# Two block products for a pair of token blocks and weight tiles: seven instead of eight, in the second projection stage of a two-layer encoder

## The chip, the cores and the metric

The kernel runs on one core of a Trainium2 chip. A core has four engines that compute, each with its own queue of instructions, worked off in order: TensorE (PE in the profile, its weight loads PEld), VectorE (DVE), ScalarE (ACT) and GpSimd (POOL). SyncE (SP) computes nothing; here it issues most of the transfers (DMA) between the chip's main memory (DRAM) and the on-chip memory SBUF. TensorE writes its results to PSUM, a second on-chip memory, from where VectorE and ScalarE read them. The metric is the device time of one execution in microseconds.

## The reference

One inference step of a two-layer encoder over 2048 prompt tokens and 32 sampled ones, 1024 features wide. Layer one is a gated DeltaNet; its result h is projected to shared keys and values and, in layer two, to queries and gates of a sliding-window attention:

```python
kv = h @ w_kv                                   # 256 key columns, 256 value columns
k  = rope_partial(kv[..., :256]); v = kv[..., 256:]
proj = h @ b_w_in                               # 1024 query columns, 1024 gate columns
q  = rope_partial(proj[..., :1024]) * 64 ** -0.5
z  = proj[..., 1024:]
o  = banded_attention(q, k, v, sinks)           # own chunk of 64 tokens and two chunks back
y  = layer_norm(4 ** 0.25 * h + (o * silu(z)) @ b_w_out, ln_g, ln_b)
```

The change is mainly in how k, q, z and v are projected, the second projection stage.

## The kernel before

All large products are made in float32 precision from pieces that TensorE reads: a tile x is split into a high part (x cast to the type fp32r, by ScalarE) and a low part (x less its high part, by VectorE or GpSimd), and x·w becomes three matmuls, high·high, high·low and low·high. `project` (L75) makes one block so: a tile of 128 weight columns, all eight slices of 128 features, a block of TB = 416 tokens, 24 matmuls into one PSUM bank. There are NB = 5 blocks of tokens; block 4 holds the end of the prompt and the 32 sampled tokens.

The order of the kernel: the first projection stage (class `P1`), the DeltaNet's chunks (`Delta`) with its output projection and layer norm beside them (`O1`), the second projection stage (class `P2`), attention (`Attention`) with its output projection, and a tail that normalises the last rows.

The second stage, as it stands before: `P2.load` (L321) fetches a block of h, transposed, from DRAM and splits it; all five blocks then lie in SBUF. Weight tiles are numbered here 0 and 1 (keys), 2 to 9 (queries), 10 to 17 (gates 0 to 7). While the last rows of the DeltaNet are projected, gates 0 and 1 of the first blocks are made; then gates 0 and 1 of blocks 2 to 4; then the values (`values`, L352): 128 tokens at a time as the stationary operand against 256 value columns, with the 32 tokens left over in each block collected over four blocks; then keys and queries (`rotated`, L1395), each with the rotation in `rope` (L1340), while the output weights of layer two are split and written to DRAM beside it (L1080); then gates 2 and 3 of all blocks and gates 4 to 7 of blocks 2 to 4. Each weight tile is fetched and split once and used on all its blocks. Eight gate blocks are left for attention's first steps, where they fill TensorE while the first scores and softmaxes run (L2053).

`rope` is, per block of 128x416: ScalarE copies from PSUM (L1345), VectorE shuffles rows (L1346), GpSimd multiplies by the sine (L1347), VectorE multiplies by the cosine (L1348) and adds (L1349). `gate` (L1422) is a tanh and a copy on ScalarE and one VectorE instruction.

What sets the order: from L2033 on the second stage is put in order by the framework's planner; attention's order (L2091) is the one written. PSUM banks come from two pools in turn (L1332).

The tail (L1605) applies mean, scale and the two tables to the last 128 rows in two halves on VectorE, after the Newton steps for the inverse deviation (L513, L515), and stores the halves.

## Time and profile before

| what | value |
| --- | --- |
| median of 3 runs (2111.22 to 2111.9) | 2111.88 us |
| profiled execution | 2112.2 us |
| its span, first to last instruction | 2110.4 us |
| TensorE busy, share of the span | 98% |
| VectorE, ScalarE, GpSimd busy | 62%, 43%, 40% |
| granted TensorE clock | 0.997 |
| moved by DMA | 307.78 MB, 145 GB/s to and from main memory |

Rows in the profile read so: a line of kernel.py (L79), the engine, the operation, output and inputs by the program's names, shapes as partitions x elements, then times. A timeline row begins with start and duration in us. Matmul durations overlap, since TensorE pipelines them; what a matmul costs in a row of them is the distance between their starts.

### The profile page before, as it was taken

The page shows a single profiled execution, that of the slowest core. Times are in us where ns is not written, and L with a number is a line of the kernel's source. Part 1 is how long each engine was busy: PE and PEld are TensorE (multiplying, and loading weights), DVE is VectorE, ACT ScalarE, POOL GpSimd, SP SyncE. Part 2 cuts the span into 40 slices and gives each one's busy share as a digit, 9 for nine tenths or more (in the row PEclk, how much of TensorE's full clock was granted, in tenths as well). Part 3 has the DMA queues.
Part 4 walks back from the last instruction along what each step waited for, and adds up shares of the span by engine and source line. Part 5 has one row for each costly group of instructions (what it writes and reads, how often), then busy time and mean ns, then how long its engine had stood idle before and what let it go on. Part 6 is the DMA issues. An engine that isn't in the chain of part 4 may idle for free.

```text
span 2110.4 us, 37218 instructions
## 1 busy us (share of the span) xinstructions
PE 2076.7 (98%) x14062; PEld 1911.9 (91%) x14062; DVE 1309.2 (62%) x2450; ACT 901.9 (43%) x2264; POOL 833.9 (40%) x1179
## 2 busy tenths in 40 slices
PE   8999999999999999999999999999999999999998
PEld 6999999999999999999988888999999997777775
DVE  4676666666557678889977886215543224666665
ACT  4444444445632377767752212312111225555552
POOL 1422232222122177777830201226443103566665
PEclk9999999999999999999999999999999999999999
DMA  5222333337665555556856764546222249534321
GB/s 206 64 69 78 115 104 98 97 117 212 194 193 165 180 155 169 169 164 209 271 168 200 237 203 121 161 161 220 91 75 73 74 111 309 140 102 120 101 72 65
DMA packets 263779, 307.78 MB, mean 146 GB/s; under 512 B 71424, under 2 KB 194624, under 8 KB 263328
## 3 DMA queue, kind: packets, MB, share of 16 engines
q1 hardware_dynamic: 252352, 281.93, 43.0%
q10 hardware_dynamic: 11248, 23.48, 3.4%
q8 instruction: 111, 1.82, 0.4%
q14 instruction: 68, 0.56, 0.1%
HBM read 189.11 MB, written 116.60 MB: 145 GB/s over the span
## 4 chain that ended last, share of the span: by engine, by line
PE 92%; DVE 3%; DMA 2%; POOL 1%; ACT 1%; issue 1%; SPq 0%; ACTq 0%; DVEq 0%; POOLq 0%
PE ps L79 17%; PE ps L81 17%; PE ps L80 17%; PE ot L1146 3%; PE ot L1147 3%; PE ot L1148 3%; PE po L1146 3%; PE po L1148 3%; PE po L1147 3%; PE S L1701 2%; PE ot L1734 2%; PE tr L1716 2%; PE g L695 1%; PE gq L831 1%; PE ks L846 1%; PE sp L846 1%
## 5 line engine op out<-in xcount | busy, mean ns | idle before, releaser
L79 PE MATMUL ps<-act_hi,w_hi 128*128 128x416 f32 x1936 | 683.1, 354 | 0.6 <-ACT act_hi L70 0.6
L81 PE MATMUL ps<-act_hi,w_lo 128*128 128x416 f32 x1936 | 681.3, 352 | 1.2 <-POOL w_lo L56 1.2
L80 PE MATMUL ps<-act_lo,w_hi 128*128 128x416 f32 x1936 | 678.2, 350 | 0.4 <-DVE act_lo L71 0.4
L79 PEld LDWEIGHTS ps<-act_hi,w_hi 128*128 128x128 f32 x1936 | 364.1, 188 | 5.8 <-ACT act_hi L70 1.3
L80 PEld LDWEIGHTS ps<-act_lo,w_hi 128*128 128x128 f32 x1936 | 363.7, 188 | 4.9 <-DVE act_lo L71 0.8
L81 PEld LDWEIGHTS ps<-act_hi,w_lo 128*128 128x128 f32 x1936 | 363.4, 188 | 5.1 <-POOL w_lo L56 1.7
L56 POOL TENSOR_TENSOR w_lo<-w_raw,w_hi 128x1024 fp32r<-128x1024 f32 x44 | 116.8, 2655 | 473.2 <-ACT w_hi L55 446.0
L209 DVE SCALAR_TENSOR_TENSOR y<-R,convw,y 128x2083 f32<-128x2083 f32 x72 | 183.0, 2542 | 62.7 <-ACT y L206 47.0
L1540 POOL TENSOR_TENSOR P<-e,sm 128x384 f32<-128x384 f32 (+2 forms) x128 | 101.2, 812 | 171.9 <-DVE sm L1530 165.9
L729 POOL TENSOR_TENSOR tm<-L,Tt 128x60 f32<-128x60 f32 (+19 forms) x365 | 133.5, 366 | 82.1 <-issue 40.5
L731 POOL TENSOR_TENSOR Tt<-Tt,tm 128x60 f32<-128x60 f32 (+19 forms) x365 | 139.7, 383 | 28.6
L1526 ACT ACTIVATE e<-S,nm 128x193 f32<-128x193 f32 (+2 forms) x260 | 104.8, 416 | 95.5 <-DVE nm L1521 58.0
L305 ACT COPY R<-ps 128x416 f32<-128x416 f32 (+1 forms) x144 | 60.3, 442 | 108.6 <-PE ps L81 95.9
L1146 PE MATMUL po<-wo_hi,g_hi 128*128 128x512 f32 x256 | 103.4, 404 | 1.0 <-DVE r L1154 0.8
L1146 PE MATMUL ot<-wo,g_hi 128*128 128x512 f32 x256 | 103.6, 405 | 0.0
L1347 POOL TENSOR_TENSOR rs<-rs,sin 128x416 f32<-128x416 f32 x50 | 70.7, 1414 | 80.4 <-DVE rs L1346 73.5
L1147 PE MATMUL ot<-wo,g_hi 128*128 128x512 f32 x256 | 101.2, 395 | 0.0
L1148 PE MATMUL ot<-wo,g_lo 128*128 128x512 f32 x256 | 100.9, 394 | 0.0
L1148 PE MATMUL po<-wo_hi,g_lo 128*128 128x512 f32 x256 | 100.2, 392 | 0.5 <-DVE g_lo L1189 0.5
L1147 PE MATMUL po<-wo_lo,g_hi 128*128 128x512 f32 x256 | 99.9, 390 | 0.0
L1432 DVE SCALAR_TENSOR_TENSOR za<-zs,za 128x416 f32<-128x416 f32 x40 | 31.7, 796 | 104.0 <-ACT za L1431 103.8
L55 ACT CAST w_hi<-w_raw 128x1024 fp32r<-128x1024 f32 x47 | 49.4, 1051 | 105.9 <-PE ps L80 73.1
(299 smaller groups left out, 3919.7 us busy)
## 6 DMA issues: line engine op xcount, KB each, us to landing
w_raw<-in_w_in SPq DMA_DIRECT2D x40, 512.0 KB
w_raw<-in_b_w_in SPq DMA_DIRECT2D x19, 512.0 KB
k<-s_k SPq DMA_DIRECT2D x17, 512.0 KB
E<-s_E SPq DMA_DIRECT2D x17, 512.0 KB
s_bz<-za SPq DMA_DIRECT2D x40, 208.0 KB
s_bq<-ra SPq DMA_DIRECT2D x40, 208.0 KB
s_q<-y SPq DMA_DIRECT2D x8, 1024.0 KB
s_wo<-wo_parts SPq DMA_DIRECT2D x16, 512.0 KB
```

The costliest lines, as they stand in the source:

```text
L56: sub.tensor_tensor(out=lo[:], in0=raw[:], in1=hi[:], op=ALU.subtract)
L79: nc.tensor.matmul(ps, hi[:, k, :], xh[:, k, :], start=(k == 0), stop=False)
L80: nc.tensor.matmul(ps, hi[:, k, :], xl[:, k, :], start=False, stop=False)
L81: nc.tensor.matmul(ps, lo[:, k, :], xh[:, k, :], start=False, stop=(k == KC - 1))
L209: nc.vector.scalar_tensor_tensor(out=y[:], in0=R[:, j:j + W], scalar=self.convw[:, i, j:j + 1], in1=y[:], op0=ALU.mult, op1=ALU.add)
L729: P.tensor_tensor(out=tm[:n, i0 - k:, :w], in0=L[:n, i0:, j:j + 1].to_broadcast(sh), in1=Tt[:n, j:j + 1, :w].to_broadcast(sh), op=ALU.mult)
L731: P.tensor_tensor(out=Tt[:n, i0:, :w], in0=Tt[:n, i0:, :w], in1=tm[:n, i0 - k:, :w], op=ALU.subtract)
L1146: nc.tensor.matmul(ps[:n], ghi[:, k, :n], hi, start=a, stop=False)
L1147: nc.tensor.matmul(ps[:n], ghi[:, k, :n], lo, start=False, stop=False)
L1148: nc.tensor.matmul(ps[:n], glo[:, k, :n], hi, start=False, stop=z)
L1526: self.nc.scalar.activation(x.e[:, h, u, :x.n], x.S[:, h, u, :], AF.Exp, bias=x.nm[:, h, u:u + 1], scale=1.0, accum_out=x.sm[:, h, u:u + 1])
L1540: self.nc.gpsimd.tensor_tensor(out=x.P[:, u, :nj * 128].rearrange("r (j h k) -> r j h k", h=2, k=64), in0=x.e[:, :, u, :n].rearrange("r h ...
```

## The change

Take two weight tiles a and b (128 columns each) and two token blocks, and cut the 1024 features into two halves. The four blocks wanted are a 2x2 matrix product with half-length sums: eight products of 12 matmuls. The change makes them from seven, by Strassen's scheme in Winograd's form: four sums of weight halves for each pair of tiles, four sums of token-block halves made once for each pair of blocks, seven products, and combinations of the results. Where products are only added up, PSUM adds them: bank A takes products 1, 3, 5 and 7 one after another, bank C products 2 and 6; between them ScalarE copies the state of a bank out (`s1`, `s5`, `s2`), and VectorE adds such a copy when a finished block is read.

Round one takes blocks 0 and 1: V, then eight pairs of tiles (keys, queries, gates 2 to 7). Then block 4 alone, all 18 tiles with 24 matmuls each as before, then V of block 4. Round two takes blocks 2 and 3: seven pairs (keys, queries, gates 0 to 3), then V. So the token blocks come and go through two places in SBUF instead of lying there all five, and the weights are fetched for each round. Gates 4 to 7 of blocks 2 and 3 go into attention's first steps, where those of blocks 0 and 1 were, and attention takes chunks 0 to 11 first, then 26 to 31, then 12 to 25. The order of all five queues in the stage is now the one written: VectorE takes over low parts of tokens and weights, results wait two steps before their last addition (`flush`), and nearly all transfers are issued by SP.

At the start of the kernel the low part of the first weight tile goes from GpSimd to VectorE, and some transfers of constants from ScalarE's queue to SP's. In the tail the mean is subtracted on ScalarE and the first table multiplied on GpSimd, beside the Newton steps on VectorE.

```diff
             if b == 1:
-                self.w0 = [split_weights(nc, self.wp, I["w_in"][i], nc.gpsimd) for i in range(2)]
+                self.w0 = [split_weights(nc, self.wp, I["w_in"][i], (nc.vector, nc.gpsimd)[i]) for i in range(2)]
...
         nc.scalar.mul(self.nwh[:], self.nwh[:], 0.5)
-        nc.scalar.dma_start(self.sel[:], I["sel"])
+        nc.sync.dma_start(self.sel[:], I["sel"])
...
+    def load(self, b, slot, sub, deep=False):
+        res = (self.resf, self.resr)[slot]
...
+        raws = [fetch(q) for q in range(4 if deep else 2)]
+        yield
...
+        for q in range(4):
+            raw, s = raws.pop(0), slice(q * 2, q * 2 + 2)
+            nc.scalar.copy(h[:, s, :], raw[:])
+            sub.tensor_tensor(out=l[:, s, :], in0=raw[:], in1=h[:, s, :], op=ALU.subtract)
+            if q < 2 and not deep:
+                raws.append(fetch(q + 2))
+            yield
+    def flush(self):
+        for f in self.older:
+            f()
+        self.older, self.later = self.later, []
...
+    def sums(self, b, deep):
...
+        parts = [[self.resl.tile([128, half, TB], F32R, tag=f"sum{i}_{c}", name="sum") for c in range(2)]
+                 for i in range(4)]
+        t1, t3, t2, t4 = parts
+        def half_of(b, i):
+            return tuple(p[:, i * half:i * half + half, :] for p in self.x[b])
+        self.seven = [lambda: half_of(b, 0), lambda: t1, lambda: t2, lambda: half_of(b, 1), lambda: t3,
+                      lambda: half_of(b + 1, 1), lambda: t4]
...
+        raws = [fetch(k) for k in range(2 if deep else 1)]
+        yield
+        for k in range(half):
+            r1, r2 = raws.pop(0)
+            b11, b12, b21, b22 = r1[:, 0], r1[:, 1], r2[:, 0], r2[:, 1]
+            for i, (out, x, y) in enumerate(((b11, b12, b11), (b12, b22, b12), (b22, b22, b11), (b21, b21, b22))):
+                V.tensor_tensor(out=out, in0=x, in1=y, op=ALU.subtract)
+                nc.scalar.copy(parts[i][0][:, k], out)
+            for i, out in enumerate((b11, b12, b22, b21)):
+                hi, lo = parts[i]
+                (nc.gpsimd if i % 2 else V).tensor_tensor(out=lo[:, k], in0=out, in1=hi[:, k], op=ALU.subtract)
+            if k + 1 + deep < half:
+                raws.append(fetch(k + 1 + deep))
+            yield
...
+        yield
+        for i, (k, c) in enumerate(todo):
+            t, raw = ahead, ahead[:, 1].bitcast(F32)
+            if i + 1 < len(todo):
+                ahead = load(i + 1)
+            nc.scalar.copy(t[:, 0], raw)
+            (nc.gpsimd, nc.vector)[c.start > 0].tensor_tensor(out=t[:, 1], in0=raw, in1=t[:, 0], op=ALU.subtract)
+            nc.sync.dma_start(kept[:, k, :, c].rearrange("a p d -> p a d"), t[:].bitcast(F32))
+            yield
...
+    def variants(self, raws):
+        nc, V, G, I = self.nc, self.nc.vector, self.nc.gpsimd, self.I
+        a, b = raws
+        out = []
+        h = KC // 2
+        a11, a12, a21, a22 = a[:, :h], a[:, h:], b[:, :h], b[:, h:]
+        s1, s2, s4 = (self.w2.tile([128, h, 128], F32, tag=f"w_sum{i}", name="w_sum", bufs=1)[:] for i in range(3))
+        V.tensor_tensor(out=s1, in0=a21, in1=a22, op=ALU.add)
+        V.tensor_tensor(out=s2, in0=s1, in1=a11, op=ALU.subtract)
+        yield out
+        V.tensor_tensor(out=a21, in0=a11, in1=a21, op=ALU.subtract)
+        V.tensor_tensor(out=s4, in0=a12, in1=s2, op=ALU.subtract)
+        yield out
+        for j, x in enumerate((a11, s1, s2, a12, a21, s4, a22)):
+            if j % 2 == 0:
+                pool = self.wp if j < 4 else self.w2
+                hi, lo = (pool.tile([128, KC, 128], F32R, tag=t, name=t) for t in ("w_hi", "w_lo"))
+            ks = slice(j % 2 * h, j % 2 * h + h)
+            nc.scalar.copy(hi[:, ks], x)
+            (V if j in (0, 3, 4) else G).tensor_tensor(out=lo[:, ks], in0=x, in1=hi[:, ks], op=ALU.subtract)
+            out.append((hi[:, ks], lo[:, ks]))
+            if j % 2 == 1 or j == 6:
+                yield out
+    def multiply(self, ps, w, x, start):
+        (hi, lo), (xh, xl) = w, x
+        h = KC // 2
+        for k in range(h):
+            for j, (u, v) in enumerate(((hi, xh), (hi, xl), (lo, xh))):
+                self.nc.tensor.matmul(ps, u[:, k, :], v[:, k, :], start=start and k == 0 and j == 0,
+                                      stop=k == h - 1 and j == 2, skip_group_check=True)
+    def pairs(self, b, units, raws, gen, w, extra):
+        nc, V = self.nc, self.nc.vector
+        for u, (ia, ib) in enumerate(units):
...
+            x = self.seven
+            def kept(ps, tag):
...
+                nc.scalar.activation(s[:], ps, AF.Copy, scale=scale)
+                return s
+            def done(i, c, ps, s):
+                a = self.wk.tile([128, TB], F32, tag="ra", bufs=4, name="ra")
+                if s is None:
+                    nc.scalar.activation(a[:], ps, AF.Copy, scale=scale)
+                else:
+                    V.scalar_tensor_tensor(out=a[:], in0=ps, scalar=scale, in1=s[:], op0=ALU.mult, op1=ALU.add)
+                self.place(i, c, a)
+            def between(m):
+                nonlocal gen, following
+                self.flush()
+                if m == 0:
+                    next(gen)
+                if m == 1:
+                    if u + 2 < len(units):
+                        raws[u % 2] = self.fetch(u, units[u + 2])
+                    if not last:
+                        gen = self.variants(raws[(u + 1) % 2])
+                        next(gen)
+                if not last:
+                    for _ in range({2: 2, 4: 1, 6: 1}.get(m, 0)):
+                        following = next(gen)
+                extra(u, m)
+            following = None
+            A, C = self.ps()[:, :TB], self.ps()[:, :TB]
+            self.multiply(A, w[0], x[0](), True)
+            between(0)
+            s1 = kept(A, "s1")
+            self.multiply(C, w[1], x[1](), True)
+            between(1)
+            s5 = kept(C, "s5")
+            self.multiply(A, w[2], x[2](), False)
+            between(2)
+            s2 = kept(A, "s2")
+            B = self.ps()[:, :TB]
+            self.multiply(B, w[3], x[3](), True)
...
+            done(ia, b, B, s1)
+            self.multiply(A, w[4], x[4](), False)
+            between(4)
+            done(ib, b + 1, A, s5)
+            self.multiply(C, w[5], x[5](), False)
+            between(5)
+            done(ia, b + 1, C, s2)
+            self.multiply(A, w[6], x[6](), False)
+            between(6)
+            done(ib, b, A, None)
+            w = following
+    def place(self, i, b, a):
+        nc, V, O, T = self.nc, self.nc.vector, self.O, self.T
...
+        s = self.wk.tile([128, TB], F32, tag="rs", name="rs")
+        if i >= 10:
+            nc.scalar.activation(s[:], a[:], AF.Tanh)
+            def gate():
+                V.scalar_tensor_tensor(out=a[:], in0=s[:], scalar=1.0, in1=a[:], op0=ALU.add, op1=ALU.mult)
+                nc.sync.dma_start(T["bz"][i - 10, :, ts], a[:])
+            self.later.append(gate)
+            return
+        cs = slice(b * TB - self.t0, b * TB - self.t0 + TB)
+        cos, sin = self.cos, self.sin
+        V.stream_shuffle(s[:], a[:], [(j + 8) % 16 if j < 16 else j for j in range(32)])
+        nc.gpsimd.tensor_tensor(out=s[:], in0=s[:], in1=sin[:, cs], op=ALU.mult)
+        V.tensor_tensor(out=a[:], in0=a[:], in1=cos[:, cs], op=ALU.mult)
...
+        def rotated():
+            V.tensor_tensor(out=a[:], in0=a[:], in1=s[:], op=ALU.add)
+            if i >= 2:
...
+    def alone(self, b, n, raws, w, extra):
+        nc = self.nc
+        for i in range(n):
+            ps = self.ps()[:, :TB]
+            drain(project(nc, ps, w, self.x[b]))
+            if i + 1 < n:
+                w = self.whole(raws.pop(0), nc.vector)
+            self.flush()
+            self.flush()
+            if i + 3 < n:
+                raws.append(self.raw((i + 3) % 2, self.source(i + 3)))
+            extra(i)
+            a = self.wk.tile([128, TB], F32, tag="ra", bufs=4, name="ra")
+            nc.scalar.activation(a[:], ps, AF.Copy, scale=1.0 if i < 2 else 0.125 if i < 10 else 0.5)
+            self.place(i, b, a)
+        self.flush()
...
+    def second_stage(self):
+        nc = self.nc
+        first = [(0, 1), *((i, i + 1) for i in range(2, 10, 2)), (12, 13), (14, 15), (16, 17)]
+        second = [*first[:5], (10, 11), (12, 13)]
+        other = self.value_raw(1, True)
+        sums = self.sums(0, 1)
+        next(sums)
+        vs = [self.half, self.value_part(other, self.w2, nc.vector)]
+        ahead = [self.fetch(u, first[u]) for u in range(2)]
+        gen = self.variants(ahead[0])
+        drain(self.gate(1, (1,), self.ps))
+        self.tables(0, 2)
+        for t, _ in enumerate(self.values((0, 1), vs)):
+            if t < 4:
+                next(sums)
...
+        def at(u, m):
+            if u >= 5 and m in (1, 3, 5) or 0 < u < 5 and m == 1:
+                next(beside, None)
+            if u + 1 < len(first):
+                return
+            if m == 1:
+                state["x"] = self.load(4, 0, nc.vector)
+                next(state["x"])
+                raws.extend(self.raw(i, self.source(i)) for i in range(2))
+            elif m >= 4:
+                next(state["x"])
...
+        self.pairs(0, first, ahead, gen, w, at)
+        self.tables(4, 1)
+        raws.append(self.raw(0, self.source(2)))
+        steps = itertools.chain(self.load(2, 1, nc.gpsimd), self.sums(2, 0))
+        held = []
+        def also(i):
+            if 2 <= i < 7 or i > 7 and i % 2 == 0:
+                next(steps)
+            if i in (11, 12):
+                held.append(self.value_raw(i - 11))
+            elif i in (13, 15):
+                held.append(self.value_part(held.pop(0), self.w2, nc.vector))
+            if i in (11, 13, 15, 17):
+                next(beside)
+        self.alone(4, 18, raws, state["w"], also)
+        drain(steps)
+        ahead = [self.fetch(u, second[u]) for u in range(2)]
+        self.tables(2, 2)
+        steps = self.load(3, 0, nc.vector, True)
+        next(steps)
+        gen = self.variants(ahead[0])
+        for t, _ in enumerate(self.values((4,), held)):
+            if t:
+                w = next(gen)
...
+        self.pairs(2, second, ahead, gen, w, at)
...
-        nc, V, n, tabs = self.nc, self.nc.vector, x.n, self.tabs
...
+        nc, V, n, tabs, pool = self.nc, self.nc.vector, x.n, self.tabs, self.otwo
+        rows = [(c, x.r[:n, c * 512:c * 512 + 512], slice(c * 512, c * 512 + 512)) for c in (1, 0)]
+        steps = self.norm(x, False)
+        next(steps)
+        nm = pool.tile([128, 1], F32, tag="nb", name="nb")
+        V.tensor_scalar(out=nm[:n], in0=x.mv[:n, 0:1], scalar1=-1.0, scalar2=None, op0=ALU.mult)
+        for c, r, cs in rows:
+            nc.scalar.activation(r, r, AF.Identity, bias=nm[:n, 0:1], scale=1.0)
+            nc.gpsimd.tensor_tensor(out=r, in0=r, in1=tabs[0][:n, cs], op=ALU.mult)
+        drain(steps)
+        for c, r, cs in rows:
+            V.scalar_tensor_tensor(out=r, in0=r, scalar=x.rs[:n, 0:1], in1=tabs[1][:n, cs], op0=ALU.mult, op1=ALU.add)
+            (nc.sync, nc.scalar)[c].dma_start(self.O["y"][x.t0:x.t0 + n, cs], r)
...
-        order = list(range(14, 32)) + list(range(14))
+        order = [*range(12), *range(26, 32), *range(12, 26)]
         last = len(order)
...
             self.stats(end, c)
-        drain(self.norm(end, False))
...
-    for b in (2, 3, 4):
-        for i in (0, 1):
-            drain(p2.gate(i, (b,), p2.ps))
-    p2.values()
-    p2.rotated()
-    for i in (2, 3):
-        p2.slab(i, nc.gpsimd)
-        drain(p2.gate(i, range(NB), p2.ps))
-    late = range(4, 8)
-    for i in late:
-        p2.slab(i, nc.gpsimd)
-        drain(p2.gate(i, (2, 3, 4), p2.ps))
+    with tc.manual_schedule(engines={ET.PE, ET.DVE, ET.Activation, ET.Pool, ET.SP}):
+        p2.second_stage()
     left.close()
     spare.close()
...
-        for m, (i, b) in enumerate(((6, 0), (7, 0), (7, 1), (4, 0), (5, 0), (4, 1), (5, 1), (6, 1))):
+        for m, (i, b) in enumerate(((6, 3), (7, 3), (7, 2), (4, 3), (5, 3), (4, 2), (5, 2), (6, 2))):
```

247 lines of the change are left out of this document (145 added, 102 removed).

## The prediction

> **What bounds the kernel now.** I read the page's busy table, slices and chain first, then TensorE's waits, then the busy times of stretches of the second projection stage.
>
> ```profile
> span 2110.4 us, 37218 instructions
> PE 2076.7 (98%) x14062; PEld 1911.9 (91%) x14062; DVE 1309.2 (62%) x2450; ACT 901.9 (43%) x2264; POOL 833.9 (40%) x1179
> PE   8999999999999999999999999999999999999998
> PEclk9999999999999999999999999999999999999999
> PE 92%; DVE 3%; DMA 2%; POOL 1%; ACT 1%; issue 1%; SPq 0%; ACTq 0%; DVEq 0%; POOLq 0%
> ```
>
> TensorE is busy for 98% of the span and carries 92% of the chain that ended last, at full clock. In the stage that is changed it is the only bound:
>
> ```profile
> core 0: us, PE busy (x) PEld busy (x) DVE busy (x) ACT busy (x) POOL busy (x), PEclk, DMA share, GB/s
> 1302.00:1784.00 482.00, 478.24 (x2779) 465.63 (x2777) 175.12 (x305) 128.63 (x285) 158.01 (x111) 1.00 0.43 136
> 1410.00:1620.00 210.00, 210.00 (x1111) 208.30 (x1111) 100.72 (x187) 40.31 (x70) 105.24 (x70) 1.00 0.36 123
> 1357.00:1389.00 32.00, 32.00 (x273) 32.00 (x272) 0.00 (x0) 5.80 (x14) 2.39 (x1) 1.00 0.32 99
> ```
>
> From 1410 to 1620 us TensorE has no gap: 210.00/1111 is 0.189 us for a matmul of 416 columns. From 1357 to 1389 us only V tiles (256 columns) run: 32.00/273 is 0.117 us. VectorE and GpSimd each stand at half. So a matmul taken away is worth 0.189 us, as long as the other engines keep up; whether they do is the question here.
>
> **What the others can do at once.** These rows hold the answer: VectorE and GpSimd instructions with their shortest, median and longest time, then places where they meet, each with start and duration.
>
> ```profile
> L1348 DVE TENSOR_TENSOR ra<-ra,cos x50: 591/593/2127, 1400.9 to 1624.1; 128x416 f32<-128x416 f32 x50
> L1346 DVE STREAM_SHUFFLE rs<-ra x50: 614/623/634, 1400.2 to 1623.5; 128x416 f32<-128x416 f32 x50
> L1154 DVE SCALAR_TENSOR_TENSOR r<-r,ot x34: 658/689/690, 1792.0 to 2100.3; 128x512 f32<-128x512 f32 x32, 32x512 f32<-32x512 f32 x2
> L56 DVE TENSOR_TENSOR w_lo<-w_raw,w_hi x3: 1224/1224/1227, 1734.5 to 1770.8; 128x1024 fp32r<-128x1024 f32 x3
> L1347 POOL TENSOR_TENSOR rs<-rs,sin x50: 1077/1427/1491, 1405.3 to 1625.5; 128x416 f32<-128x416 f32 x50
> L1093 POOL TENSOR_TENSOR wo_parts<-wo_parts x16: 1287/1292/1302, 1396.0 to 1469.7; 128x512 fp32r<-128x512 f32 x16
> L71 POOL TENSOR_TENSOR act_lo<-act_raw,act_hi x12: 1976/1995/2830, 1170.5 to 1321.9; 128x832 fp32r<-128x832 f32 x12
> 1424.24 2.41 POOL L56 TENSOR_TENSOR w_lo<-w_raw,w_hi 128x1024 fp32r<-128x1024 f32 x1
> 1424.32 0.63 DVE L1346 STREAM_SHUFFLE rs<-ra 128x416 f32<-128x416 f32 x1
> 1424.99 2.11 DVE L1348 TENSOR_TENSOR ra<-ra,cos 128x416 f32<-128x416 f32 x1
> 1426.60 1.44 POOL L1347 TENSOR_TENSOR rs<-rs,sin 128x416 f32<-128x416 f32 x1
> 79.71 4.67 DVE L209 SCALAR_TENSOR_TENSOR y<-R,convw,y 128x2083 f32<-128x2083 f32 x2
> 80.62 13.42 POOL L56 TENSOR_TENSOR w_lo<-w_raw,w_hi 128x1024 fp32r<-128x1024 f32 x1 [0.95 <-ACT w_hi L55]
> 89.26 2.37 DVE L209 SCALAR_TENSOR_TENSOR y<-R,convw,y 128x2083 f32<-128x2083 f32 x1
> 91.56 0.21 DVE L388 TENSOR_SCALAR gtmp<-gtmp 128x136 f32<-128x136 f32 x1
> ```
>
> At 1424.99 a VectorE product of two SBUF tiles waits until GpSimd's subtraction ends at 1426.65 and ends 0.45 us after that; the GpSimd product issued at 1426.60 then takes 1.44 instead of 1.08. They exclude each other. The shuffle at 1424.32, with one input, isn't touched, nor is the addition from PSUM (L1154, 658 to 690 in all 34). At 80.62 GpSimd asks, and waits until 91.6, when VectorE's row of two-input instructions ends: VectorE keeps its turn while its next instruction is ready. So a VectorE two-input instruction of 416 columns holds for 0.45 us; one of 512 for 0.55, since the rows at 416 and 1024 columns differ by 631 ns over 608. GpSimd holds for 1.08 and 1.29.
>
> **The change part by part.** *Matmuls.* In two of three rounds a pair of weight tiles times a pair of token blocks takes 7 products of 12 matmuls in place of 4 blocks of 24: 84 for 96. There are 8 + 7 such units, so 180 matmuls x 0.189 = 34.0 us go. V has 18 tiles instead of 17, since leftover tokens aren't collected over four blocks: 24 x 0.117 = +2.8. TensorE alone: **-31.2 us**.
>
> *A rotary unit (5 in each round).* TensorE: 84 x 0.189 = 15.9 us (18.1 before). GpSimd: four low parts and four sine products, 4 x 1.29 + 4 x 1.08 = 9.5. VectorE with two SBUF inputs: four weight sums, three low parts, four cosine products, four additions, 7 x 0.55 + 8 x 0.45 = 7.5. These exclude each other, so the unit cannot take less than 17.0; TensorE is late by 1.1 at least. I then laid both queues out as written. VectorE's own work, spaced as in its rows, is 7 x 0.64 + 8 x 0.54 + 4 x 0.62 + 3 x 0.57 = 13.0 us. It waits for GpSimd about 4.7: 1.0 before the second cosine product (a low part has just begun), 0.4 before the last, 2.4 before the last addition (its sine product stands behind a low part that VectorE itself had kept out), 1.2 behind the next low part. So 17.7, **1.8 over TensorE**. TensorE feels it where product 7 writes over the PSUM tile that VectorE's combination after product 5 reads: one product, 2.3 us, lies between, and about 1.6 us of that is slack, once a round. Ten units: 10 x 1.8 - 2 x 1.6 = 14.8. In three units of the first round a piece of the output weights comes on top, two on GpSimd, one on VectorE: 2 x 1.29 + 0.64 = 3.2. Sum **+18.0**; ends +11 (17.0 a unit) and +42 (all in turn, below).
>
> *A gate unit (3 + 2).* No sine, one VectorE addition for each block: 4 x 1.29 + 7 x 0.55 + 4 x 0.45 = 10.8, with three output-weight pieces about 14 of 15.9. Covered by TensorE; costs nothing. Between 0 and 1 a unit.
>
> *The lone block (18 tiles x 4.5 us).* VectorE now makes each low part (1.22) beside shuffle, product and addition; with GpSimd's 1.08 that is 4.5 us from a block's end, in time. In four blocks block 2 is also split, 832 columns on GpSimd (1.99), and stands ahead of the addition: a period of 5.7 instead of 4.5, four times, less 1.9 slack: **+2.9** (0 to 5). The later sums fall into gate blocks, 8.7 of 9.1 us for two: +0.5.
>
> *Seams.* Start: the first sums need four rounds of loads, VectorE, ScalarE and GpSimd, under seven V tiles (19.8 us); the third weight's low part is about 1 late. First round to lone block: the last quarter of block 4, 0.5. Second round: four splits on VectorE in its first unit, 0.5. **+2.0** (0 to 10, since no row shows these loads in this order).
>
> *The queues.* SP issues nearly all; the weights come three times, some 15 MB more, the sums read 7 MB again: 22 MB in 450 us on top of 136 GB/s is 185, and weights are asked for a unit ahead. A store that waits for a late addition holds back the weight load behind it on SP by those 2 us of 15.9: nothing. ScalarE: per unit seven high parts, three copies out, one combination, under 8 of 15.9. It adds one wait: the copy after product 3 stands behind the high part of a sum of VectorE's; by my layout TensorE needs it 0.5 us later than it comes when VectorE is late, less than the delay counted already.
>
> *The attention order (chunks 0 to 11 first).* Same products; eight gate blocks still lie under its first loads. Its first iterations are smaller. The one wait of TensorE's there was 1.2; +-1, taken as 0.
>
> *The two ends:*
>
> ```profile
> PE ps L81 <- POOL w_lo L56: 1.2, 1, 1.2
> 12.59 2.37 POOL L56 TENSOR_TENSOR w_lo<-w_raw,w_hi 128x1024 fp32r<-128x1024 f32 x1 [11.38 <-ACT w_hi L55]
> 2101.78 0.21 DVE L1582 BATCH_NORM_AGGREGATE mv<-st 128x2 f32<-128x12 f32 x1
> 2104.07 0.21 DVE L515 TENSOR_SCALAR ln_y<-ln_t,ln_y 128x1 f32<-128x1 f32 x1
> 2104.20 0.74 DVE L1609 SCALAR_TENSOR_TENSOR r<-r,mv,ln_g 128x512 f32<-128x512 f32 x1
> 2106.43 0.75 DVE L1611 SCALAR_TENSOR_TENSOR r<-r,ln_y,ln_b 128x512 f32<-128x512 f32 x1
> ```
>
> In front VectorE makes the low part in 1.22 instead of 2.37: of the 1.2 us that TensorE waits, **-1.1**. Late next is the following block's data, from a DMA. The constants moved onto SP stand behind loads there; ScalarE's first use of one could come late: between -1.5 and +1. At the end mean and first table are applied on ScalarE and GpSimd under the Newton steps (2101.78 to 2104.28), so VectorE's four steps of 0.75 become two; GpSimd's second half (1.29 twice after two ScalarE halves) ends near 2105.4, one product after it 2106.15 for 2107.18: **-1.0** (-1.5 to 0).
>
> *Sum:* -31.2 + 18.0 + 2.9 + 0.5 + 2.0 - 1.1 - 1.0 = **-9.9 us**. The profiled run took 2112.2, 0.3 above the median of the runs; so 2102.3 there, **2102.0 us** as a median.
>
> [...]
>
> **The rivals.** *A: the gain arrives whole.* If VectorE's fixed part (0.14 of 0.59 us) and unused turns absorb the exclusion, TensorE stays the bound: -31.2 - 2.1 + 2, **2081**. For it: each engine alone has room (9.5 and 13.0 of 15.9). Against it: the rows above exclude in every meeting, and 17.0 is over 15.9.
>
> *B: turns in order of request.* Then GpSimd also gets in between VectorE's bursts of sums, and nearly each of its eight instructions stops VectorE: laid out so, a rotary unit takes 20.1, 4.2 over TensorE: 10 x 4.2 - 3.2 + 3.2 = 42.0 for 18.0, **2126**, slower. For it: at 1426.60 a GpSimd instruction gave way to the one that had waited longer. Against it: 80.62. From 18.7 us a rotary unit on (9.9 / 10 over 17.7), the change loses.
>
> *C: the seams.* Loads and sums of two changes of blocks come late one after another, 10 us instead of 2: **2111**, no change. For it: before, all blocks lay in SBUF and TensorE waited for splits 1 us in all. Against it: V tiles cover the start and the second round.
>
> **How the numbers follow.** Forecast (a rotary unit at 17.0 to 18.3 gives 2095 to 2108; with the bounds of the small terms 2092 to 2110) 0.52, A (2078 to 2092) 0.20, B (2112 to 2135) 0.18, C 0.10. A measurement of this kernel tells about 0.2%, 4.2 us, from no change. Faster: 0.20 and most of the forecast, 0.45, 0.65 in all; within 0.2%: 0.07 of the forecast, 0.06 of C, 0.02 of B, 0.15; slower 0.20. The range leaves out half of A below and half of B above: 2083 to 2125; the likeliest's own is 2092 to 2110.
>
> **What would show it.** TensorE's matmuls fall by 156, 180 less in products. In rotary units of the pair rounds TensorE has gaps of about 2 us a unit before the seventh product, put down to VectorE; VectorE's two-input products and GpSimd's sine products show means far over 0.59 and 1.08; in gate units there are no gaps. Wrong: gaps in rotary units near 0 (A) or 4 us (B), or gaps that stand at the seams (C).

## The result and the profile after

The changed kernel takes 2162.25 us (median of four runs, 2157.54 to 2163.92) against 2111.89 for the kernel before in the same comparison: a ratio of 1.023, 95% interval 1.022 to 1.024. It is slower by 50 us; the forecast was 10 us faster. The profiled execution took 2157.54 us, 45.3 above that of before.

The page of the changed kernel, its span, busy times and two of its rows of slices:

```profile
span 2155.7 us, 37623 instructions
PE 2068.6 (96%) x13906; PEld 1888.8 (88%) x13906; DVE 1544.0 (72%) x2681; ACT 985.2 (46%) x2411; POOL 909.7 (42%) x1232
PE   8999999999999999999999998888888899999998
PEclk9999999999999999999999999999999999999999
```

TensorE has 156 matmuls fewer, just as forecast, and yet the span is longer. Its busy time fell by 8 us only, where the matmuls that are gone were worth 31; so some of the others took longer. The section on the clock below shows which. The page alone would not alarm anyone: 96% busy, and a row of eights where nines stood.

The waits of TensorE in the changed kernel (releasing engine and line, us in total, times, longest) name the place:

```profile
PE ps L1459 <- ACT part L1472: 21.6, 11, 3.2
PE ps L1459 <- DVE ra L1480: 17.0, 10, 3.0
PE ps L81 <- DVE w_lo L1560: 7.5, 9, 2.4
PE ps L79 <- ACT w_hi L1559: 5.3, 4, 2.2
```

The products of the pair rounds (L1459) wait in the rotary units above all: in eight of the ten before product 5 for ScalarE's copy of the accumulator, in six before product 7 for VectorE's combination. The lone block waits for its weights. In the kernel before, TensorE's waits in this stage (1302.0 to 1721.7) came to 1.7 us in all, the longest 0.7.

Busy time of TensorE in the stretches of the second stage, in order: V of blocks 0 and 1, the five rotary units of round one, its three gate units, the lone block, V of block 4, the rotary units of round two, its two gate units, V of blocks 2 and 3. The first two numbers are the stretch and its length; then busy time, matmuls, granted clock.

```profile
core 0: us, PE busy (x), PEclk, DMA share, GB/s
1314.34:1338.74 24.40, 21.68 (x169) 0.93 0.87 307
1338.74:1443.56 104.82, 87.96 (x424) 0.93 0.34 113
1443.56:1502.39 58.83, 50.21 (x252) 0.97 0.62 212
1502.39:1602.28 99.89, 88.56 (x432) 0.97 0.69 229
1602.28:1613.35 11.07, 11.07 (x98) 1.00 0.89 325
1613.35:1713.18 99.83, 85.75 (x422) 0.97 0.33 113
1713.18:1749.03 35.85, 32.20 (x167) 1.00 0.25 86
1749.03:1770.15 21.12, 19.92 (x169) 1.00 0.43 137
```

Each stretch can be held against what its matmuls need in an unbroken row (0.189 us each at 416 columns, 0.117 for V, from the kernel before; 84 matmuls a unit, 24 a tile):

| stretch | length | needed | over | forecast |
| --- | --- | --- | --- | --- |
| ten rotary units | 204.65 | 158.8 | 45.9 | 18.0 |
| five gate units | 94.68 | 79.4 | 15.3 | 0 |
| lone block | 99.89 | 81.6 | 18.3 | 3.4 |
| three stretches of V (seams) | 56.59 | 50.5 | 6.1 | 2.0 |

In all 85.6 us over, where 23.4 were forecast. Four things have to be taken off: the 31.2 of fewer matmuls, 1.7 that TensorE lost in this stage before (419.67 us from 1302.03 to 1721.70, 417.97 of them busy), 3.1 that the attention and the end are shorter now (385.5 from the stage's end to the last instruction, 388.7 before) and 2.5 by which the stage begins earlier (its first gate block at 1299.56, before at 1302.03). That leaves +47.1 for the 45.3 measured; 0.001 us in the price of a matmul, taken over some 2000 of them, would make the rest.

**A rotary unit.** VectorE starts a unit's first sum at 1662.70 and the next unit's at 1682.50: 19.8 us, TensorE needs 15.9. Timeline rows (start, duration) of VectorE and of GpSimd in that unit of the changed kernel:

```profile
1664.02 0.68 DVE L1439 TENSOR_TENSOR w_raw<-w_raw 128x512 f32<-128x512 f32 x1
1664.62 1.79 DVE L1440 TENSOR_TENSOR w_sum<-w_raw,w_sum 128x512 f32<-128x512 f32 x1
1668.22 0.59 DVE L1543 TENSOR_TENSOR ra<-ra,cos 128x416 f32<-128x416 f32 x1
1668.73 1.57 DVE L1448 TENSOR_TENSOR w_lo<-w_raw,w_hi 128x512 fp32r<-128x512 f32 x1
1682.50 0.68 DVE L1436 TENSOR_TENSOR w_sum<-w_raw 128x512 f32<-128x512 f32 x1
```

```profile
1664.11 1.76 POOL L1448 TENSOR_TENSOR w_lo<-w_sum,w_hi 128x512 fp32r<-128x512 f32 x1 [1.78 <-ACT w_hi L1447]
1668.34 1.42 POOL L1542 TENSOR_TENSOR rs<-rs,sin 128x416 f32<-128x416 f32 x1 [2.47 <-DVE rs L1541]
```

GpSimd asks at 1664.11, in the middle of a row of VectorE's sums. It doesn't have to wait for the end of that row: VectorE's next sum, begun at 1664.62, takes 1.79 instead of 0.68. The same at 1668.34, when a cosine product is running. Over the whole stage (instruction, count, shortest, median and longest time in ns):

```profile
L1546 DVE TENSOR_TENSOR ra<-ra,rs x50: 578/1476/2373, 1360.3 to 1720.5; 128x416 f32<-128x416 f32 x50
L1542 POOL TENSOR_TENSOR rs<-rs,sin x50: 1406/1426/1497, 1356.6 to 1718.7; 128x416 f32<-128x416 f32 x50
L1541 DVE STREAM_SHUFFLE rs<-ra x50: 615/626/643, 1355.9 to 1717.9; 128x416 f32<-128x416 f32 x50
L1480 DVE SCALAR_TENSOR_TENSOR ra<-ps,part x45: 576/578/593, 1355.2 to 1746.8; 128x416 f32<-128x416 f32 x45
```

GpSimd's sine product waits for the rest of one VectorE instruction at most (1.41 to 1.50 us for 1.08 in all fifty; in the kernel before its median was the same), while half of VectorE's additions take 1.48 or more instead of 0.58. Shuffle and combination, with one SBUF input, are untouched (615 to 643 and 576 to 593 ns in all). This is the order of rival B.

**The clock.** In the second stage of the changed kernel the trace has nine stretches at half the clock, eight of 3.41 us and one of 6.83 (1346.60 to 1353.43), each beginning a whole number of 3.41 us after the one before it: ten windows of 3.41 us. Three pairs of consecutive ones of this length (busy time, matmuls, clock):

```profile
1343.19:1346.60 3.41, 0.65 (x2) 0.99 0.12 40
1346.60:1350.01 3.41, 2.09 (x6) 0.50 0.69 201
1459.24:1462.66 3.42, 1.55 (x9) 1.00 0.47 169
1462.66:1466.07 3.41, 2.30 (x12) 1.00 0.61 223
1701.59:1705.00 3.41, 1.63 (x9) 0.99 0.61 193
1705.00:1708.41 3.41, 3.41 (x12) 0.51 0.66 239
```

A window in which TensorE was busy for 0.65 or 1.63 us is followed by one at half the clock, one with only 1.55 us by one at full clock. Eleven windows of the stage hold at most 1.63 us of work. Nine of them are followed by the half clock, but two, with 1.55 (at 1459.24) and 1.61 us (at 1722.07), by the full one. So in this stage little work in a window mostly stood ahead of a half-speed one, but the busy time as the profile models it gives no sharp limit. A half-speed window full of work costs, as an estimate from its clock of 0.51, half of 3.41, 1.7 us of matmuls, so the ten make at most 17 of the 23 us that TensorE's busy time is above what 31.2 us of matmuls fewer would leave; the rest isn't placed.

### The profile page after: what moved, and what is told of

The parts are those of the page before. It is cut to its first block, busy times and chain, and to the rows that moved or that the text cites. A ratio compares the mean times of both kernels' runs of the same rounds, so it can differ in the third digit from the quotient of the medians.

```text
span 2155.7 us, 37623 instructions
## 1 busy us (share of the span) xinstructions
PE 2068.6 (96%) x13906; PEld 1888.8 (88%) x13906; DVE 1544.0 (72%) x2681; ACT 985.2 (46%) x2411; POOL 909.7 (42%) x1232
## 5 line engine op out<-in xcount | busy, mean ns | idle before, releaser
L81 PE MATMUL ps<-act_hi,w_lo 128*128 128x416 f32 x1456 | 515.0, 354 | 7.5 <-DVE w_lo L1560 7.5
L79 PE MATMUL ps<-act_hi,w_hi 128*128 128x416 f32 x1456 | 516.6, 355 | 5.4 <-ACT w_hi L1559 5.3
L80 PE MATMUL ps<-act_lo,w_hi 128*128 128x416 f32 x1456 | 510.8, 351 | 0.6 <-DVE act_lo L1338 0.6
L81 PEld LDWEIGHTS ps<-act_hi,w_lo 128*128 128x128 f32 x1456 | 274.2, 188 | 13.3 <-DVE w_lo L1560 10.7
L79 PEld LDWEIGHTS ps<-act_hi,w_hi 128*128 128x128 f32 x1456 | 274.3, 188 | 10.7 <-ACT w_hi L1559 6.7
L80 PEld LDWEIGHTS ps<-act_lo,w_hi 128*128 128x128 f32 x1456 | 274.5, 189 | 4.9 <-DVE act_lo L1338 0.9
L56 POOL TENSOR_TENSOR w_lo<-w_raw,w_hi 128x1024 fp32r<-128x1024 f32 x27 | 77.2, 2860 | 376.3 <-ACT w_hi L55 348.4
L1459 PE MATMUL ps<-sum,w_hi 128*128 128x416 f32 x480 | 138.1, 370 | 39.5 <-ACT part L1472 21.6
L1834 ACT ACTIVATE e<-S,nm 128x193 f32<-128x193 f32 (+2 forms) x260 | 104.6, 415 | 95.1 <-DVE nm L1829 56.5
L1459 PEld LDWEIGHTS ps<-sum,w_hi 128*128 128x128 f32 x480 | 92.1, 196 | 49.0 <-ACT part L1472 25.4
L1147 PE MATMUL po<-wo_lo,g_hi 128*128 128x512 f32 x256 | 99.9, 390 | 0.0
```

The costliest lines, as they stand in the source:

```text
L79: nc.tensor.matmul(ps, hi[:, k, :], xh[:, k, :], start=(k == 0), stop=False)
L80: nc.tensor.matmul(ps, hi[:, k, :], xl[:, k, :], start=False, stop=False)
L81: nc.tensor.matmul(ps, lo[:, k, :], xh[:, k, :], start=False, stop=(k == KC - 1))
L1147: nc.tensor.matmul(ps[:n], ghi[:, k, :n], lo, start=False, stop=False)
L1459: self.nc.tensor.matmul(ps, u[:, k, :], v[:, k, :], start=start and k == 0 and j == 0, stop=k == h - 1 and j == 2, skip_group_check=True)
L1834: self.nc.scalar.activation(x.e[:, h, u, :x.n], x.S[:, h, u, :], AF.Exp, bias=x.nm[:, h, u:u + 1], scale=1.0, accum_out=x.sm[:, h, u:u + 1])
```

## The experiments

Theory T: VectorE's two-input instructions and GpSimd's exclude each other, turn by turn, and VectorE sets the rotary unit's 19.8 us. Rival S: the order on ScalarE's queue, on which the larger of TensorE's waits is put down. Also to settle: whether the half-speed windows cost much, and what the gate units, the lone block and the seams lost.

**e1: the block products stay in PSUM.** Behind the combination, shuffle, cosine product, addition and gate product read the block from its PSUM bank, in the lone block too:

```diff
-                a = self.wk.tile([128, TB], F32, tag="ra", bufs=4, name="ra")
+                a = self.ps()[:, :TB] if (i, c) == (ib, b + 1) else ps
...
-        V.tensor_tensor(out=a[:], in0=a[:], in1=cos[:, cs], op=ALU.mult)
+        V.tensor_tensor(out=a, in0=a, in1=cos[:, cs], op=ALU.mult)
...
-            V.tensor_tensor(out=a[:], in0=a[:], in1=s[:], op=ALU.add)
+            r = self.wk.tile([128, TB], F32, tag="ra", bufs=4, name="ra")
+            V.tensor_tensor(out=r[:], in0=a, in1=s[:], op=ALU.add)
...
```

> Edit: in the pair rounds and the lone block the finished block product stays in PSUM (in place, one bank more a unit), so that shuffle, cosine product, addition and the gate's product each read at most one SBUF tile; same operations on the same engines. Theory T (VectorE and GpSimd exclude each other on VectorE instructions with two SBUF inputs, and this sets a rotary unit's 19.8 us): VectorE's two-SBUF instructions fall from 15 to 7 a rotary unit, hold 7.5 -> 3.9 us, the cosine product's median comes back to 0.6 us, the unit falls to 16.0 to 17.0, and the whole from 2162 to about 2122 (2105 to 2140). Rival S (the order on ScalarE's queue sets the unit: the copy after product 3 stands behind the high part of a sum): the unit stays within 0.5 of 19.8, the whole 2150 to 2165.

Measured: 2111.46 us, 0.998 of before (0.997 to 0.999). With the same instructions on the same engines 51 us are gone. The groups of addition, sine product and cosine product, and TensorE's time over five units of round two (four rotary units and the first gate unit), of e1:

```profile
L1548 DVE TENSOR_TENSOR ra<-ps,rs x50: 566/578/593, 1363.3 to 1676.6; 128x416 f32<-128x416 f32 x50
L1543 POOL TENSOR_TENSOR rs<-rs,sin x50: 1075/1089/2077, 1360.1 to 1675.5; 128x416 f32<-128x416 f32 x50
L1544 DVE TENSOR_TENSOR ps<-ps,cos x50: 587/597/602, 1359.9 to 1674.8; 128x416 f32<-128x416 f32 x50
1609.83:1689.56 79.73, 79.73 (x422) 1.00 0.32 110
```

The addition falls from 1476 to 578 ns in the median, the sine product from 1426 to 1089, and five units take 79.73 us without a gap: 15.95 each, TensorE's own time. (The cosine product, named in the expectation, had not been slow: 593 ns in the median before e1 too.) Theory T holds for the settled units. From first matmul to first matmul, the ten rotary units fall from 104.6 and 99.6 us to 88.5 and 84.2, so 31.5 of the 45.9 lost there are gone; most of the 14 left is in the first unit of each round (23.5 and 20.4 us). The gate units, whose product had two SBUF inputs as well, gain 10 us (59.0 and 36.2 to 53.0 and 32.0), the lone block 5.5 (99.9 to 94.4).

**e2: the copy first.**

```diff
-            between(2)
             s2 = kept(A, "s2")
+            between(2)
```

> Edit: the ScalarE copy after product 3 is issued ahead of the next unit's high parts instead of behind them. Theory T: the waits before product 5 (21.6 us in all) mostly go, but VectorE still needs 19.8 us a rotary unit, so the time comes back before product 7: the whole 2152 to 2165. Rival S: 7 of 10 units lose 3 us of wait, the whole about 2141.

Measured: 2165.5 us (1.024 of before, 1.022 to 1.026). The waits for ScalarE's copies went from 21.6 to 3.2 us in all, those for VectorE's combination rose from 17.0 to 32.3. Removing a wait that the profile names gained nothing, because the engine behind it was late with the next thing. S falls.

**e3: no sine product.**

```diff
-        nc.gpsimd.tensor_tensor(out=s[:], in0=s[:], in1=sin[:, cs], op=ALU.mult)
+        if b == NB - 1:
+            nc.gpsimd.tensor_tensor(out=s[:], in0=s[:], in1=sin[:, cs], op=ALU.mult)
```

> Left out: the sine product of the rotation in the pair rounds (the shuffled tile is added unmultiplied; the lone block keeps it). Theory T: GpSimd has 4 x 1.08 us less in a rotary unit and VectorE stops for it four times less; the unit falls from 19.8 to 16.0 to 17.0, the whole to about 2127 (2115 to 2138). Rival S: under 5 us, since ScalarE's queue is the same: 2157 to 2165.

Measured: 2116.72 us; the rotary units of round two, behind the first, take 15.95 us (1611.59 to 1675.38 for four). Four GpSimd instructions fewer take 3.8 us out of a unit, all that TensorE's 15.9 allows: VectorE had been paying for them. The time is within what theory T gave; rival S had under 5 us.

**e4: the two ends alone, on the kernel before.**

```diff
-                self.w0 = [split_weights(nc, self.wp, I["w_in"][i], nc.gpsimd) for i in range(2)]
+                self.w0 = [split_weights(nc, self.wp, I["w_in"][i], (nc.vector, nc.gpsimd)[i]) for i in range(2)]
...
-        drain(self.norm(end, False))
         self.tail(end)
```

with the tail and the moved constants as in the change.

> Edit: the kernel before with only the change's front and tail (first low part on VectorE, constants on SP's queue, the last normalisation spread over three engines). If front and tail do what the prediction said: -1.1 and -1.0, about 2109.8 (2107 to 2112), so that all of the loss and more lies in the second projection stage. If the moved constants cost something, at or above 2112.

Measured: 2110.23 us, 0.998 of before (0.997 to 0.9995). The ends gain. VectorE's last rows, first before, then e4:

```profile
2101.78 0.21 DVE L1582 BATCH_NORM_AGGREGATE mv<-st 128x2 f32<-128x12 f32 x1
2106.43 0.75 DVE L1611 SCALAR_TENSOR_TENSOR r<-r,ln_y,ln_b 128x512 f32<-128x512 f32 x1
```

```profile
2099.86 0.21 DVE L1582 BATCH_NORM_AGGREGATE mv<-st 128x2 f32<-128x12 f32 x1
2102.55 2.29 DVE L1617 SCALAR_TENSOR_TENSOR r<-r,ln_y,ln_b 128x512 f32<-128x512 f32 x2
```

From the aggregate to the end 5.40 us become 4.98. The tail gives 0.4 of the forecast 1.0: GpSimd's products run until 2103.62, and VectorE's two last ones, each with two SBUF inputs, take 2.29 us together where one alone took 0.75. The front's wait of 1.2 is gone. These rows give 1.6 us; by the medians the gain lies between 1 and 6.

**e5: the form of VectorE's instructions.** The forecast's order rested on one row of the front, where instructions that read a column of scalars kept GpSimd out for 11 us. Here the second stage's have that form:

```diff
+    def two(self, out, in0, in1, op):
+        self.nc.vector.scalar_tensor_tensor(out=out, in0=in0, scalar=self.one[:, 0:1], in1=in1, op0=ALU.mult, op1=op)
```

> Edit: the changed kernel with VectorE's two-SBUF sums, low parts, cosine products and additions of the second stage written as scalar_tensor_tensor with a column of ones as scalar, the form of the front's instruction that kept GpSimd out from 80.62 on; values unchanged. Theory K (an instruction that also reads a column keeps VectorE's turn, and so the order that the prediction took would hold here): the rotary unit falls from 19.8 to about 17.7, the whole from 2162 to about 2141 (2130 to 2150), with single GpSimd instructions of over 3 us. Rival L (the form doesn't matter; who asked first is next): the unit stays within 0.5 of 19.8, the whole 2155 to 2172.

Measured: 2169.19 us; the unit is 20.3 us, each instruction some 0.06 us longer. GpSimd gets in as before: at 1733.92 one of VectorE's sums takes 1.85 us, the next 0.74. The form is not it.

**e6: needless matmuls in the gaps.**

```diff
+    def fill(self, F, w, x, ia):
+        for k in range(8 if ia < 10 else 0):
+            self.nc.tensor.matmul(F, w[0][:, k % 4, :], x[0][:, k % 4, :], start=True, stop=True, skip_group_check=True)
```

> Edit: the changed kernel with eight needless matmuls (1.5 us) before product 5 and again before product 7 of each rotary unit, into a PSUM bank of their own: 160 matmuls, 30 us of TensorE's time. If VectorE and GpSimd set the rotary unit, they lie in TensorE's waits: the unit stays at 19.8, TensorE has no half-speed window in the rotary units any more, and the whole is 2154 to 2163. If TensorE's own time or its order sets the unit, the whole rises towards 2192.

Measured: 2161.56 us (1.023 of before). TensorE over four units of round two, the changed kernel first, then e6 (there from one first sum of VectorE to the fourth after it):

```profile
1633.85:1713.18 79.33, 69.08 (x338) 0.96 0.29 97
```

```profile
1647.84:1727.00 79.16, 79.14 (x416) 1.00 0.29 97
```

TensorE does 78 matmuls more in the same time, at full clock, and is busy for 79.14 of 79.16 us without setting the pace. Its own unit, now 100 matmuls, takes 18.96 us (starts at 1641.47, 1660.43, 1679.39, 1698.35), while VectorE's first sums stay 19.79 apart; so 64 of the 78 are the added ones, the others come from running ahead, and at 1728.79 TensorE waits again. The time of the kernel is the same with the added work: the half-speed windows inside the rotary units cost nothing. Those at the seams and in the lone block, where TensorE itself is late, would be the ones to pay for; no run takes them out alone.

**e7 and e8: on e1, all copies first; then the lone block's first splits earlier.**

```diff
+            s1 = kept(A, "s1")
             between(0)
-            s1 = kept(A, "s1")
...
+            elif m == 2:
+                state["w"] = self.whole(raws.pop(0), nc.vector)
             elif m >= 4:
                 next(state["x"])
-                if m == 5:
-                    state["w"] = self.whole(raws.pop(0), nc.vector)
-                elif m == 6:
+                if m == 4:
                     next(state["x"])
```

(the first half in both, the second in e8)

> Edit: e1_psum with all three ScalarE copies of a unit issued ahead of the next high parts. In e2 alone this gave nothing, since VectorE set the unit; with VectorE relieved the wait of 3.2 us before product 3 of the first unit and the half-speed window behind it should go: 2111.5 to about 2106.5 (2104 to 2109). If VectorE is still the bound there, no change: 2110 to 2113.

> Edit: e7 and, in the last unit of the first round, the lone block's first weight tile split after product 3 instead of 6 and block 4's quarters split after products 5 (two), 6 and 7 instead of 5, 6 and 7 (two). If the lone block's slow start (waits of 4.5 us in all at 1483 to 1491 of e1, and 6.8 us at half speed after them) comes from these splits alone, 5 to 8 us less than e7, about 2100 (2097 to 2104). If the loads of block 4 set it, within 1.5 us of e7.

Measured: e7 2111.46 us (0.999, 0.9985 to 1.0004), e8 2114.2 (1.001, 0.9998 to 1.002). Neither gained. In e7 the units of round one are shorter, but the first unit of round two takes 23.1 us instead of 20.4: TensorE waits there 2.6 us for the weights' low part, as in e1, and 2.0 more for VectorE before product 7. Why VectorE is later there is open. In e8 the lone block is shorter (89.0 us for 93.6), but the last unit of round one takes 25.3 us instead of 19.1, because the split that was put earlier stands on ScalarE's queue before its weights have landed. ScalarE in e8:

```profile
1474.39 1.04 ACT L1561 CAST w_hi<-w_raw 128x1024 fp32r<-128x1024 f32 x1 [7.13 <-DMA w_raw<-in_w_k]
```

Behind it VectorE's combination is late, and TensorE waits 7.6 us before product 7.

**e9 and e10: four loads asked for earlier, on e7 and on the changed kernel.**

```diff
+            if u + 2 == len(first) and m == 1:
+                raws.extend(self.raw(i, self.source(i)) for i in range(2))
...
+            if i == 16:
+                self.par = 1
+                state["ahead"] = self.fetch(0, second[0])
```

and V's second half of weights on ScalarE's queue, the lone block's first split behind product 3.

> Edit: e7 and four loads asked for earlier: the second half of V's weights on ScalarE's queue instead of behind stores on SP's, the lone block's first two weight tiles a unit earlier (and the first split after product 3), the second round's first pair of weights in the lone block's tile 17. In e7 these places cost TensorE waits of 2.1 + 0.8 (V), 2.3 + 0.8 (lone block), 2.6 (second round) and three half-speed windows of 3.4 us. If late requests cause them, 8 to 12 us go: 2111.5 to about 2101 (2098 to 2105). If they come from VectorE's backlog there, under 3 us: 2108 to 2112.

> Edit: the changed kernel with the four earlier loads of e9 alone. The rotary units stay at 19.8 (VectorE and GpSimd set them), so only the seams gain: 2162 to about 2154 (2150 to 2158). If late loads rather than the exclusion were the main loss, more than 20 us.

Measured: e9 2103.91 us, 0.996 of before (0.994 to 0.997); e10 2152.51 (1.019, 1.017 to 1.021). The two differences to the kernels without it, 7.6 and 9.7 us, agree: this part of the loss is late requests, independent of the exclusion. e9 is 10 us faster than the kernel before, 0.4%. What it still loses, by stretches (V with 0.6 us of the gate block ahead of it, rotary and gate units of round one, the lone block):

```profile
1315.00:1335.85 20.85, 20.37 (x172) 1.00 0.89 302
1335.85:1421.80 85.95, 81.61 (x420) 0.98 0.41 140
1421.80:1473.22 51.42, 48.40 (x254) 1.00 0.69 235
1473.22:1566.99 93.77, 86.00 (x433) 0.98 0.77 256
```

The lone block is still 12 us over its 81.6, half of it in its first two tiles, where block 4 is being split. No run tries to mend that.

**e11 and e12: what decides whose turn it is.** In e11 the front's VectorE products are cut into pieces of 417 columns, on the kernel before; in e12 the second stage's two-input instructions are cut in half, on the changed kernel.

```diff
-            nc.vector.scalar_tensor_tensor(out=y[:], in0=R[:, j:j + W], scalar=self.convw[:, i, j:j + 1], in1=y[:],
-                                           op0=ALU.mult, op1=ALU.add)
+            for a in range(0, W, 417):
+                z = min(a + 417, W)
+                nc.vector.scalar_tensor_tensor(out=y[:, a:z], in0=R[:, j + a:j + z], scalar=self.convw[:, i, j:j + 1],
+                                               in1=y[:, a:z], op0=ALU.mult, op1=ALU.add)
```

```diff
+        self.first_half(*a, op)
+        self.second_half(*b, op)
```

> Edit: the kernel before with the front's convolution products on VectorE (2083 columns, 2.37 us each) cut into five pieces of at most 417 columns, the size of the second stage's instructions; values unchanged. Question: why GpSimd's low part at 80.62 waited 11 us. Theory D (it is the length of VectorE's instructions): GpSimd gets in after one or two pieces, and its 128x1024 low parts of the front all take under 4 us. Rival E (in a row of ready two-input instructions VectorE keeps the turn whatever their length): some of them still take 8 us or more. The time itself rises by the pieces' fixed parts, some 0.1 us for each of 384 more instructions where VectorE is the bound, 0 to 20 us.

> Edit: the changed kernel with each of VectorE's two-SBUF sums, low parts, cosine products and additions of the second stage issued as two instructions, one after another, for the two halves of its columns; values unchanged. The second half depends on nothing that the first did not already wait for. In e11 a row of ten short pieces kept a GpSimd copy out for 5.58 us, here GpSimd gets in each time; Theory W (GpSimd gets in where VectorE's next instruction carries a wait for another engine, even one long fulfilled): second halves all take their lone time, under 0.6 us, and only first halves are long. Theory X (it gets in at any boundary): second halves of over 1.2 us are as frequent as first halves. In both the rotary unit rises from 19.8 by about 1 us of fixed parts, the whole to about 2172 (2162 to 2185).

Measured: e11 2120.19 us (1.0045, 1.002 to 1.007), e12 2172.11 (1.028, 1.025 to 1.031). In e11 no low part took over 2.8 us, as theory D wants; but the ask of 80.62 fell elsewhere, and another row speaks against D. VectorE, then GpSimd, in e11:

```profile
230.52 5.70 DVE L211 SCALAR_TENSOR_TENSOR y<-R,convw,y 128x417 f32<-128x417 f32 x10
```

```profile
230.69 5.58 POOL L302 COPY R<-convs 128x3 f32<-128x3 f32 x1
```

Ten short pieces run without a break, and a copy of three columns waits for the last of them. So here VectorE kept its turn over a row of short instructions. In e12 both happen within one unit. VectorE, then GpSimd:

```profile
1641.59 0.37 DVE L1322 TENSOR_TENSOR ra<-ra,cos 128x208 f32<-128x208 f32 x1
1641.89 1.26 DVE L1325 TENSOR_TENSOR ra<-ra,cos 128x208 f32<-128x208 f32 x1
```

```profile
1641.64 1.27 POOL L1562 TENSOR_TENSOR rs<-rs,sin 128x416 f32<-128x416 f32 x1 [1.86 <-DVE rs L1561]
1654.57 3.11 POOL L1468 TENSOR_TENSOR w_lo<-w_sum,w_hi 128x512 fp32r<-128x512 f32 x1 [2.48 <-ACT w_hi L1464]
```

At 1641.64 GpSimd gets in between the two halves of one product, which theory W excludes. The second half of the cosine product shows it all fifty times:

```profile
L1325 DVE TENSOR_TENSOR ra<-ra,cos x50: 1232/1255/1277, 1355.9 to 1732.4; 128x208 f32<-128x208 f32 x50
```

At 1654.57 it waits 1.8 us, through a row of five half-size sums and low parts, which theory X excludes. Form, length of the single instruction and a wait carried by the next one are each ruled out as the whole answer; what decides it stays open. For this kernel it is enough that, uncut, GpSimd got in almost every time.

## Why the prediction was wrong

*The step that failed* is the sentence "VectorE keeps its turn while its next instruction is ready". It was read from the row at 80.62 and carried to instructions at another place; from it came 17.7 us for a rotary unit. The runs put 19.8 in its place, with GpSimd in between VectorE's instructions as in rival B, which had 20.1. The term for the rotary units was 18.0 and measured 45.9. In e1, with less to exclude, 31.5 of it go, and in e1 and e3 the settled units come down to TensorE's 15.95; the other 14 lie mostly in the first unit of each round. The row at 1426.60, quoted for rival B, was the nearer one: same stage, same kind and size of instruction. The prediction set it aside for a single row of the front.

*That alone gives rival B's 2126; nearly all of the other 36 us is in three terms that were too small.* Gate units: 0 forecast, 15.3 measured. They were costed by the exclusive time of both engines added up (10.8 of 15.9), with no waits in it and no backlog from the rotary unit ahead; e1 takes 10 of it away. Lone block: 3.4 forecast, 18.3 measured. Its weights were said to be "in time" with 4.5 us from a block's end; TensorE waited 12.8 us for their high and low parts. e1 takes 5.5 away, so the exclusion is a part of it; e8, which splits earlier, takes 5 more out of the block and pays for them in the unit before; 12 are left in e9, and what makes them is shown only for the first two tiles. V and the seams: 2.0 forecast, 6.1 measured, of which e9 takes V's first stretch from 24.40 to 20.23 us (1315.62 to 1335.85).

*The clock was left out.* The sum had no term for the half-speed windows, which followed nine of the eleven windows with little work. e6 shows that in the rotary units they are free (2161.56 us with the gaps filled, 2162.25 with the half-speed windows). That the windows at the seams cost half of 3.41 us each is the author's estimate from the clock of 0.51, not separately measured.

*Small slips* that change nothing in the outcome: the four waits named for VectorE in a rotary unit add up to 5.0, not 4.7; rival C's sum gives 2110, not 2111.

*What was right:* 156 matmuls fewer; the exclusion itself, and that one-input instructions are untouched; the gap before product 7 put down to VectorE (the one before product 5 had been taken as covered); the gain of the front (1.2 for 1.1). The tail gave 0.4 for 1.0. DMA capacity was not the limit of the rotary units (share 0.33).

*Of the rivals:* A's 2081 would need TensorE to be the bound; in e1 it is in the rotary units of round two behind the first, and e9, at 2103.91, is still 23 us away from it: 12 over in the lone block, and most of the rest in the first unit of each round (22.5 and 19.7 us for 15.9) and in the gate units. C was a part of the loss (7.6 and 9.7 us in e9 and e10), not a case of its own.

## What to carry to other kernels

When work moves from TensorE to VectorE and GpSimd, count VectorE's instructions with two SBUF inputs and GpSimd's as one queue, and charge most of GpSimd's time to VectorE unless rows of the same kind, size and place show otherwise: here VectorE's unit was 6.8 us longer than the 13.0 estimated for its own work, for 9.5 us of GpSimd's instructions. The cheapest cure here was where a tile lies: leaving a product in PSUM took 51 us off without touching a single operation's engine. And a wait that the profile names is worth removing only if the engine behind it is not late anyway (e2), or if the data it then needs has been asked for (e7, e8, e9).

## What the runs showed of the hardware

- TensorE's clock changed by windows of 3.41 us in the second stage of the changed kernel; ten were at half speed (0.50 to 0.51). Nine of eleven windows with 0.65 to 1.63 us of work were followed by one at half speed, two with 1.55 and 1.61 us were not; waits of 1.8 us came out both ways (half speed at 1705.00, full at 1725.48).
- TensorE was busy for 79.14 of 79.16 us and did not set the pace (e6: TensorE's unit 18.96 us, VectorE's 19.79).
- Whether GpSimd got in between two ready VectorE instructions varied: nearly always with 416 to 512 columns in the second stage (at most 1.50 us for a sine product of 1.08, 2.15 for a low part of 1.29); not once in a row of ten pieces of 417 columns in the front (e11, 5.58 us for a 128x3 copy); both with 208 and 256 columns (e12).
- VectorE wrote and read PSUM tiles as fast as SBUF ones here: the cosine product took 597 ns in PSUM and 593 alone in SBUF.
